# w_down of a SwiGLU layer as seven block products: hidden kept as seven pieces, half of the results added by accumulating transfers

## The chip, the cores and the metric

The kernel runs on one NeuronCore of a Trainium2 chip. The metric is the device time of one execution in microseconds (us), as a median of several runs. The engines are named as the profile names them: PE is TensorE (PEld its weight loads), DVE is VectorE, ACT is ScalarE, POOL is GpSimd, SP is SyncE, which here only starts DMA transfers.

## The reference, cut to what matters

One inference step of a hybrid encoder of two layers over 656 tokens, with a model width of 1024 and a feed-forward width of 2816, all in fp32. Each layer is a SwiGLU, a mixer (pooling, convolution, attention) and a second SwiGLU:

```python
def swiglu(x, w_gate, w_up, w_down):
    return (jax.nn.silu(x @ w_gate) * (x @ w_up)) @ w_down

h   = x + 0.5 * swiglu(rmsnorm(x, g1), ...)     # SwiGLU 1
h   = h + mixer(rmsnorm(h, gm))
out = h + 0.5 * swiglu(rmsnorm(h, g2), ...)     # SwiGLU 2
```

There are four SwiGLUs in all. The change concerns their last product, the one by `w_down` (2816 x 1024).

## The kernel before

**Layout.** Everything stands transposed: features on the 128 partitions, tokens along the free axis. The 656 tokens are worked in two halves of 328 (the last SwiGLU drops 16 tokens and has halves of 320). The feed-forward width is 22 tiles of 128, taken as 11 pairs; `H` holds the residual as 8 tiles `m` of 128 features.

**Products in fp32.** `mm3` makes one fp32 product from three matmuls in the faster fp32r format: each operand is split into a high and a low part (`split`: ACT copies the high part, DVE subtracts it to get the low one), and high times high, high times low and low times high are summed in PSUM. In the profile all these matmuls have one line, L143, and differ by the PSUM tile that they write: `mm` (2 buffers), `z` (4) or `aux` (2).

**Units.** The program is a list of units. Each loads weights into `raw` or `rawb` by SP's DMA queue, splits them into slabs (`prep_next`: ACT the high part, DVE the low one; a slab is 4 blocks of 128x128, hence the operations of 128x512), and runs matmuls. `pump`, called after each product, loads and splits ahead, as buffers come free. The order in which each engine then takes its instructions is set by a scheduler that simulates the time line.

**Gate and up** are pair units (`pair_unit`, `run_pair`). Two tiles of output features, two halves of the tokens and two halves of the 1024 inputs make a 2x2 by 2x2 block product, which is made in seven block products instead of eight, as Strassen and Winograd do: 7 x 12 = 84 matmuls. The seven combined inputs (`B11`, `B12`, `B21`, `B22`, `Q1`, `Q2`, `T3`, `T4`) stand in `XR`; `mix` makes the combinations with four DVE operations. The combined weights are made by two accumulating transfers (`grow`: a DMA that POOL issues and that adds to what its destination holds) and two DVE additions. Results are put together by ACT and DVE. The last product, `T4`, is not run in its own unit: `self.late` keeps it, and the next unit runs it behind its own first product.

**Down, before.** `w_down` is worked in four chunks of 2, 3, 3 and 3 pairs (`CHUNKS`). `up_out` multiplies silu(gate) by up and splits each tile of the hidden layer into `Ra` (in the profile `ra`): one split of 656 tokens for each of the pair's two tiles. When a chunk is complete, 8 plain units (`hu_down`, one for each `m`) each make, for each half of the tokens, one sum in a `z` bank over the chunk's tiles, 3 matmuls a tile, and DVE adds it to `H` (`H<-z`). The list puts a chunk's eight down units behind the next chunk's first gate unit:

```python
                units.append(self.pair_unit(g[l], f, self.gate_out))
                units += down
                down = []
                units.append(self.pair_unit(up[l], f, self.up_out, i=2 * i))
```

So the order is: ..., up unit of the chunk's last pair, gate unit of the next pair, the eight down units, up unit of that pair. The up unit's `T4`, on which the last hidden tile waits, runs within that gate unit. Behind it come `mul`, and the split of that tile.

## Time and profile before

| | |
|---|---|
| Runs | 2853.79, 2850.09, 2853.23 us, median 2853.23 us |
| The profiled execution | 2852.38 us, of which the trace's span is 2850.7 us |
| PE busy | 2821.5 us, 99% of the span |
| DVE busy | 1853.5 us, 65% |
| ACT busy | 1320.7 us, 46% |
| POOL busy | 222.5 us, 8% |
| PE's waits for other work | 26 us in 13 groups |
| Mean granted TensorE clock | 0.994 |

The share of an engine is its busy time by the span, and an average over stages. Matmuls are pipelined, and the mean of one that a group gives covers its whole passage (312 ns), which overlaps with its neighbours; what a matmul costs is a full stretch of PE by the number of matmuls in it.

### The profile page before, as it was taken

How to read it: one execution, taken by the hardware profiler on the slowest of the kernel's cores; microseconds unless marked ns; L12 is line 12 of the kernel's file. 1: busy time of each engine (PE TensorE's matmuls, PEld its weight loads, DVE VectorE, ACT ScalarE, POOL GpSimd, SP SyncE). 2: the span in 40 equal slices, each digit the busy share in tenths (PEclk: the TensorE clock that was granted, in tenths of full speed). 3: DMA queues.
4: the chain of work that ended last, by engine and by line, in shares of the span. 5: the costliest groups of instructions: out<-in, count | busy, mean ns of one | idle time of the engine just before them, and what ended most of it. 6: DMA issues, size and time to landing. Idle time of an engine off the chain costs nothing.

```text
span 2850.7 us, 48269 instructions
## 1 busy us (share of the span) xinstructions
PE 2821.5 (99%) x19179; PEld 2781.3 (98%) x19179; DVE 1853.5 (65%) x3422; ACT 1320.7 (46%) x2544; POOL 222.5 (8%) x321
## 2 busy tenths in 40 slices
PE   8999999999999999999999999999999999999999
PEld 7999999999999999999999999999999999999999
DVE  8676675876444776575776665758764456775764
ACT  6353454776333343353554443547763234443443
POOL 1001000011000001000010010001110001000010
PEclk8999999999999999999999999999999999999999
DMA  5445444222222445454445454442222225444452
GB/s 148 115 128 120 120 113 99 80 78 70 75 71 71 101 116 138 107 128 117 123 105 131 122 128 103 109 100 81 68 77 71 74 76 134 111 121 117 126 124 73
DMA packets 506772, 297.26 MB, mean 104 GB/s; under 512 B 14430, under 2 KB 481570, under 8 KB 506546
## 3 DMA queue, kind: packets, MB, share of 16 engines
q1 hardware_dynamic: 478692, 241.87, 29.5%
q0 software_dynamic: 27360, 51.98, 10.6%
q8 instruction: 150, 2.46, 0.3%
q14 instruction: 76, 0.62, 0.1%
q10 hardware_dynamic: 494, 0.32, 0.0%
HBM read 233.84 MB, written 8.31 MB: 85 GB/s over the span
## 4 chain that ended last, share of the span: by engine, by line
PE 96%; DMA 2%; DVE 1%; ACT 1%; issue 0%; POOL 0%; ACTq 0%; SPq 0%; DVEq 0%; POOLq 0%
PE z L143 59%; PE mm L143 36%; PE aux L143 1%; DMA Wa<-rawb 0%; DMA raw<-in_ffn_w_gate_dram 0%; DVE Wa L131 0%; DMA raw<-in_ffn_w_up_dram 0%; DVE XR L134 0%; PE aux L1088 0%; DMA rawb<-in_ffn_w_gate_dram 0%; DMA rawb<-rawb 0%; ACT Wa L120 0%; DVE ws L134 0%; PE aux L1068 0%; DMA Wa<-in_k_norm_dram 0%
## 5 line engine op out<-in xcount | busy, mean ns | idle before, releaser
L143 PE MATMUL mm<-XR,ws 128*128 128x328 f32 (+3 forms) x4848 | 800.8, 314 | 2.1 <-DVE Wa L134 2.1
L143 PEld LDWEIGHTS mm<-XR,ws 128*128 128x128 f32 x4848 | 738.6, 188 | 7.0 <-issue 2.9
L143 PE MATMUL z<-XR,ws 128*128 128x328 f32 (+3 forms) x3924 | 628.5, 312 | 7.5 <-ACT XR L120 6.6
L143 PEld LDWEIGHTS z<-XR,ws 128*128 128x128 f32 x3924 | 596.2, 189 | 9.0 <-ACT XR L120 7.2
L143 PE MATMUL z<-ra,ws 128*128 128x328 f32 (+1 forms) x2688 | 421.0, 311 | 1.4 <-DVE H L131 1.4
L120 ACT ACTIVATE ws<-raw 128x512 fp32r<-128x512 f32 (+1 forms) x429 | 264.2, 618 | 324.0 <-PE z L143 206.5
L143 PEld LDWEIGHTS z<-ra,ws 128*128 128x128 f32 x2688 | 405.1, 188 | 1.7 <-DVE H L131 1.7
L134 DVE TENSOR_TENSOR ws<-raw,ws 128x512 fp32r<-128x512 f32 (+1 forms) x429 | 287.9, 673 | 176.7 <-ACT ws L120 175.3
L143 PE MATMUL z<-ra,slabs 128*128 128x328 f32 (+1 forms) x2112 | 330.3, 312 | 0.0
L143 PEld LDWEIGHTS z<-ra,slabs 128*128 128x128 f32 x2112 | 319.3, 188 | 0.1
L143 PE MATMUL mm<-XR,slabs 128*128 128x328 f32 (+1 forms) x1944 | 316.4, 312 | 0.0
L143 PE MATMUL z<-XR,slabs 128*128 128x328 f32 (+1 forms) x1764 | 297.0, 315 | 7.3 <-DVE Wa L134 7.3
L143 PEld LDWEIGHTS mm<-XR,slabs 128*128 128x128 f32 x1944 | 296.5, 188 | 0.0
L143 PEld LDWEIGHTS z<-XR,slabs 128*128 128x128 f32 x1764 | 274.3, 191 | 8.0 <-DVE Wa L134 7.9
L134 DVE TENSOR_TENSOR Wa<-Wa 128x328 f32<-128x328 f32 (+5 forms) x325 | 215.2, 668 | 36.4 <-ACT Wa L120 33.0
L131 DVE SCALAR_TENSOR_TENSOR H<-z,H 128x328 f32<-128x328 f32 (+1 forms) x288 | 140.9, 493 | 143.5 <-PE z L143 143.2
L120 ACT ACTIVATE slabs<-raw 128x512 fp32r<-128x512 f32 (+1 forms) x183 | 109.4, 601 | 160.4 <-PE z L143 78.0
L120 ACT ACTIVATE Wa<-Wa 128x656 f32<-128x656 f32 (+7 forms) x232 | 136.9, 597 | 92.5 <-DVE Wa L134 88.6
L120 ACT ACTIVATE ws<-rawb 128x512 fp32r<-128x512 f32 (+1 forms) x183 | 109.5, 601 | 147.3 <-PE z L143 94.2
L120 ACT ACTIVATE Wa<-mm 128x328 f32<-128x328 f32 (+1 forms) x240 | 105.5, 439 | 148.9 <-PE mm L143 147.9
L120 ACT ACTIVATE slabs<-rawb 128x512 fp32r<-128x512 f32 (+1 forms) x181 | 107.6, 599 | 143.8 <-PE z L143 99.3
L134 DVE TENSOR_TENSOR ws<-rawb,ws 128x512 fp32r<-128x512 f32 (+1 forms) x183 | 118.8, 652 | 61.0 <-ACT ws L120 60.1
(177 smaller groups left out, 2552.8 us busy)
## 6 DMA issues: line engine op xcount, KB each, us to landing
raw<-in_w_in_dram SPq DMA_DIRECT2D x88, 512.0 KB, 3.7
raw<-in_ffn_w_gate_dram SPq DMA_DIRECT2D x57, 512.0 KB, 4.0
rawb<-in_ffn_w_up_dram SPq DMA_DIRECT2D x55, 512.0 KB, 4.5
rawb<-in_ffn_w_down_dram SPq DMA_DIRECT2D x48, 384.0 KB, 3.3
raw<-in_ffn_w_down_dram SPq DMA_DIRECT2D x48, 384.0 KB, 3.4
raw<-in_ffn_w_up_dram SPq DMA_DIRECT2D x33, 512.0 KB, 3.9
rawb<-in_ffn_w_gate_dram SPq DMA_DIRECT2D x31, 512.0 KB, 3.5
Wa<-in_ffn_w_gate_dram SPq DMA_DIRECT2D x40, 256.0 KB, 3.9
```

Of the source, the lines that this page charges most:

```text
L120: i = self.nc.scalar.activation(out, in_, func, **kw).ins
L131: return self.nc.vector.scalar_tensor_tensor(out, in0, scalar, in1, op0=op0, op1=op1).ins
L134: self.nc.vector.tensor_tensor(out, in0, in1, op=op)
L143: self.nc.tensor.matmul(out, lhsT, rhs, start=start, stop=stop, skip_group_check=True)
```

## The change

**Chunks.** There are five chunks, of 2, 2, 2, 2 and 3 pairs. The last is done as before. The `w_down` of the first four is done by seven block products.

**Down units.** For a chunk of two pairs, tiles `m` and `m + 4` of the output, the two halves of the tokens and the two tiles of each pair make the 2x2 by 2x2 blocks. A `down_unit` (four to a chunk, for m = 0 to 3) runs 7 products of 2 x 3 = 6 matmuls, 42 in all, in three banks, where two plain units for the same outputs ran 48. Its last product, `T4`, is kept as `late` too. Its weights are four SP transfers of 128 KB and one more (`a21`), two accumulating transfers, two DVE additions of 128x256, and slabs of 4, 4, 4 and 2 blocks.

**Results.** The two blocks of tile `m` are the sum of two banks each: ACT takes a bank times 0.5 into one of six buffers (`terms`), and an accumulating transfer adds that to `H` (`first`, four times a unit). The blocks for `m + 4` are added by DVE as before (`second`, with factor -0.5, three times a unit).

**Hidden.** Of each pair the hidden layer is kept as seven pieces. `up_out` does, when the pair is complete: a split of one block of 328, a split of two (656), `mix` (four DVE operations of 328), and a split of four blocks (1312), where there were two splits of 656.

The diff, cut to its core:

```diff
-CHUNKS = ((0, 2), (2, 3), (5, 3), (8, 3))
+CHUNKS = ((0, 2), (2, 2), (4, 2), (6, 2), (8, 3))
...
+    def down_unit(self, w, r0, l, m):
+        part = lambda r, m: w[r0:r0 + 4 * P, m * P:(m + 1) * P].rearrange("(i r p) c -> r p i c", r=2, p=P)[r]
+        parts = [(4 * c + 2 * r, 2, part(r, m + 4 * c)) for c in range(2) for r in range(2)]
+        return dict(slabs=[4, 4, 4, 2], src=[(KD, parts)], placed=True, prep=self.prep_down, then=self.sums_down,
+                    early=self.early_down, run=self.run_down, ring="F", s3n=1, m=m, l=l, a21=part(0, m + 4))
...
+    def early_down(self, u):
+        (_, A), = u["raw"]
+        self.nc.sync.dma_start(u["s3"], u["a21"])
+        self.grow(A[:, 4:6], A[:, 6:8])
+        self.grow(u["s3"], A[:, 0:2])
+
+    def sums_down(self, u, i):
+        if i == 1:
+            (_, A), = u["raw"]
+            self.tt(A[:, 0:2], A[:, 4:6], A[:, 0:2], ALU.add)
+            self.tt(A[:, 2:4], A[:, 0:2], A[:, 2:4], ALU.add)
...
+        def first(hi, bank):
+            t = self.terms[self.term_i % 6][:, :n]
+            self.term_i += 1
+            self.act(t, bank[:, :n], AF.Identity, scale=0.5)
+            self.grow(h[0][hi], t)
+
+        def second(hi, bank):
+            self.stt(h[1][hi], bank[:, :n], -0.5, h[1][hi], ALU.mult, ALU.add)
+
+        plain = self.use(u)
+        prod(b1, plain, 0, B11, True)
+        first(0, b1)
+        self.pump(1)
+        if self.late:
+            self.late()
+        s1 = self.use(u)
+        prod(b2, s1, 0, Q1, True)
+        second(1, b2)
...
+        prod(b3, plain, 1, B21, True)
+        first(0, b3)
...
+        prod(b1, s2, 0, Q2, False)
+        first(1, b1)
...
+        prod(b2, s2, 1, B22, False)
+        first(1, b2)
...
+        prod(b1, s3, 0, T3, False)
+        second(1, b1)
...
+        def last():
+            self.late = None
+            prod(b1, s1, 1, T4, False)
+            second(0, b1)
...
-            for m in SLOTS:
-                down.append(self.unit(k, [(0, k, dn[l][r0:r0 + k * P, m * P:(m + 1) * P])], self.hu_down, "F",
-                                      m=m, l=l, scale=0.5, to=to if ci == len(CHUNKS) - 1 else None,
-                                      last=ci == len(CHUNKS) - 1))
+            if final:
...
+            else:
+                down = [self.down_unit(dn[l], r0, l, m) for m in range(4)]
...
     def up_out(self, u, r, n):
         s, w = (a[:, 2 * n * r:2 * n * (r + 1)] for a in (self.sil, self.up))
         self.mul(w, w, s)
-        self.split(self.r_at(0, u["i"] + r, c.start, c.stop), self.r_at(1, u["i"] + r, c.start, c.stop), w)
+        b = [self.up[:, q * n:(q + 1) * n] for q in range(4)]
+        if r == (1 if "plain" in u else 0):
+            self.split(self.hid(0, i, B11, n), self.hid(1, i, B11, n), b[0])
+        if r:
+            self.split(self.hid(0, i, B21, n, 2), self.hid(1, i, B21, n, 2), w)
+            self.mix(*b)
+            self.split(self.hid(0, i, Q2, n, 4), self.hid(1, i, Q2, n, 4), self.up[:, :4 * n])
```

**Where it moves instructions.** The first place is PE, at the first chunk's down products in the first SwiGLU. `mm_735` (before) and `mm_741` (after) is the bank of the up unit's last product T4; `mm_856` and `mm_874` are banks of the gate unit that follows; rows with `ra_550` are down products. Before:

```order
L143 MATMUL mm_735<-XR,slabs_104 128x328 x12
L143 MATMUL mm_856<-XR,ws_815 128x328 x12
L143 MATMUL z_857<-XR,ws_835 128x328 x12
L143 MATMUL z_984<-ra_550,slabs_104 128x328 x9
L143 MATMUL z_1022<-ra_550,slabs_104 128x328 x2
L143 MATMUL mm_856<-XR,ws_853 128x328 x12
L143 MATMUL z_984<-ra_550,slabs_104 128x328
L143 MATMUL z_1022<-ra_550,slabs_104 128x328
L143 MATMUL z_984<-ra_550,slabs_104 128x328 x2
```

And after, again from T4 on:

```order
L147 MATMUL mm_741<-XR,slabs_104 128x328 x12
L147 MATMUL mm_874<-XR,ws_871 128x328 x12
L147 MATMUL mm_1018<-XR,slabs_104 128x328 x6
L147 MATMUL z_1020<-ra_550,slabs_104 128x328 x3
L147 MATMUL z_1094<-ra_550,ws_1013 128x328 x3
L147 MATMUL z_1095<-ra_550,ws_995 128x328 x3
L147 MATMUL z_1020<-ra_550,slabs_104 128x328
L147 MATMUL z_1095<-ra_550,ws_995 128x328
L147 MATMUL mm_874<-XR,slabs_104 128x328 x12
L147 MATMUL z_1020<-ra_550,slabs_104 128x328 x2
L147 MATMUL z_1095<-ra_550,ws_995 128x328 x2
L147 MATMUL mm_1018<-ra_550,slabs_104 128x328 x3
```

What follows right behind:

```order
L147 MATMUL mm_1093<-XR,ws_995 128x328 x6
L147 MATMUL mm_1093<-ra_550,ws_1029 128x328 x3
L147 MATMUL z_1019<-ra_550,slabs_104 128x328
L147 MATMUL mm_1018<-ra_550,slabs_104 128x328
L147 MATMUL z_1094<-ra_550,ws_1013 128x328
L147 MATMUL mm_1093<-ra_550,ws_1029 128x328
L147 MATMUL z_1019<-ra_550,slabs_104 128x328 x2
L147 MATMUL mm_1018<-ra_550,slabs_104 128x328 x2
L147 MATMUL z_1094<-ra_550,ws_1013 128x328 x2
```

Before, the first product that needs the newest low part of the hidden tile is the last row (`z_984` x2). After, the first that needs the newest pair's high parts of `mix` is the third row of the second piece (`z_1019`), and of its low parts the seventh. Between T4 and the row in question stand 49 matmuls before and 61 after (52 before the high part's row).

The second place is DVE, from the evict of the same T4 to the newest low part. Before:

```order
L131 SCALAR_TENSOR_TENSOR Wa<-mm_735,Wa 128x328
L134 TENSOR_TENSOR slabs_104<-rawb_105,slabs_104 128x512
L134 TENSOR_TENSOR Wa<-Wa 128x656
L134 TENSOR_TENSOR ra_550<-Wa,ra_550 128x656
L134 TENSOR_TENSOR Wa<-z_857,Wa 128x328
```

After, first half and second half:

```order
L135 SCALAR_TENSOR_TENSOR Wa<-mm_741,Wa 128x328
L138 TENSOR_TENSOR slabs_104<-rawb_105,slabs_104 128x512
L138 TENSOR_TENSOR Wa<-Wa 128x656
L138 TENSOR_TENSOR rawb_105<-rawb_105 128x256
L138 TENSOR_TENSOR ws_1029<-rawb_105,ws_1029 128x512
L138 TENSOR_TENSOR rawb_105<-rawb_105 128x256
L138 TENSOR_TENSOR ra_550<-Wa,ra_550 128x656
L138 TENSOR_TENSOR Wa<-Wa 128x328
L138 TENSOR_TENSOR slabs_104<-rawb_105,slabs_104 128x512
L138 TENSOR_TENSOR Wa<-Wa 128x328
```

```order
L135 SCALAR_TENSOR_TENSOR Wa<-Wa 128x328
L138 TENSOR_TENSOR Wa<-Wa 128x328
L135 SCALAR_TENSOR_TENSOR Wa<-mm_874,Wa 128x328
L138 TENSOR_TENSOR slabs_104<-Wa,slabs_104 128x256
L135 SCALAR_TENSOR_TENSOR Wa<-Wa 128x328
L138 TENSOR_TENSOR slabs_104<-raw_914,slabs_104 128x512
L135 SCALAR_TENSOR_TENSOR Wa<-Wa 128x328
L138 TENSOR_TENSOR raw_914<-raw_914 128x256
L138 TENSOR_TENSOR ws_1132<-Wa,ws_1132 128x256
L138 TENSOR_TENSOR raw_914<-raw_914 128x256
L138 TENSOR_TENSOR ra_550<-Wa,ra_550 128x1312
```

The newest low part is the last row with `ra_550`: the fourth instruction from T4's evict before, the twenty-first after, because the mix, the sums of the down units' weights and their splits now stand between.

The third place is POOL, which issues the accumulating transfers, in the same SwiGLU. Before, each pair unit's two are the only ones:

```order
L410 DMA Wa<-rawb_105 128x512
L410 DMA rawb_105<-rawb_105 128x512
L410 DMA Wa<-raw_1036 128x512
L410 DMA raw_1038<-raw_1038 128x512
L410 DMA Wa<-rawb_105 128x512
```

After, the down units' sums (128x256) and the results (`H<-Wa`) come in:

```order
L445 DMA Wa<-raw_922 128x256
L445 DMA raw_922<-raw_922 128x256
L445 DMA H<-Wa 128x328
L445 DMA rawb_105<-rawb_105 128x512
L445 DMA H<-Wa 128x328 x2
L445 DMA Wa<-rawb_105 128x512
L445 DMA H<-Wa 128x328 x6
L445 DMA Wa<-raw_1204 128x512
L445 DMA raw_1206<-raw_1206 128x512
L445 DMA H<-Wa 128x328 x7
```

A pair unit's transfers (128x512) now stand among 16 transfers into `H` a chunk, four for each of its four down units.

## Rows read from the trace of the kernel before

**Rows 1.** The page: busy time of each engine, and the granted clock in 40 slices

```profile
PE 2821.5 (99%) x19179; PEld 2781.3 (98%) x19179; DVE 1853.5 (65%) x3422; ACT 1320.7 (46%) x2544; POOL 222.5 (8%) x321
...
PEclk8999999999999999999999999999999999999999
```

**Rows 2.** The page: the chain that ended last, by engine and by line

```profile
PE 96%; DMA 2%; DVE 1%; ACT 1%; issue 0%; POOL 0%; ACTq 0%; SPq 0%; DVEq 0%; POOLq 0%
```

**Rows 3.** PE's waits: us in total, times, longest us

```profile
PE z L143 <- DVE Wa L134: 7.3, 2, 4.1
PE z L143 <- ACT XR L120: 6.6, 2, 5.5
PE aux L143 <- ACT Wa L120: 2.9, 1, 2.9
...
PE z L143 <- DVE H L131: 1.4, 1, 1.4
```

**Rows 4.** Windows over one chunk, its two parts, and chunks of other SwiGLUs

```profile
core 0: us, PE busy (x) PEld busy (x) DVE busy (x) ACT busy (x) POOL busy (x), PEclk, DMA share, GB/s
128.60:247.80 119.20, 119.20 (x795) 119.20 (x795) 76.76 (x134) 50.27 (x94) 9.41 (x11) 1.00 0.48 119
128.60:210.00 81.40, 81.40 (x544) 81.40 (x544) 61.63 (x104) 41.94 (x80) 5.98 (x7) 1.00 0.48 120
210.00:247.80 37.80, 37.80 (x253) 37.80 (x252) 15.12 (x30) 8.33 (x14) 3.43 (x4) 1.00 0.49 116
1098.30:1217.50 119.20, 119.20 (x794) 119.20 (x793) 77.22 (x134) 50.19 (x94) 9.53 (x11) 1.00 0.48 119
2505.40:2621.60 116.20, 116.20 (x795) 116.20 (x794) 76.33 (x133) 49.95 (x94) 9.55 (x11) 1.00 0.48 122
```

**Rows 5.** DVE's groups, shapes apart

```profile
L134 DVE TENSOR_TENSOR ws<-raw,ws 128x512 fp32r<-128x512 f32 x405 | 278.2, 688 | 174.2 <-ACT ws L120 172.8
...
L134 DVE TENSOR_TENSOR Wa<-Wa 128x656 f32<-128x656 f32 x130 | 108.7, 836 | 1.5
...
L131 DVE SCALAR_TENSOR_TENSOR H<-z,H 128x328 f32<-128x328 f32 x208 | 102.1, 495 | 94.1 <-PE z L143 94.0
...
L134 DVE TENSOR_TENSOR ra<-Wa,ra 128x656 fp32r<-128x656 f32 x66 | 55.2, 836 | 12.3 <-ACT ra L120 12.3
L134 DVE TENSOR_TENSOR Wa<-Wa 128x328 f32<-128x328 f32 x92 | 45.6, 496 | 26.6 <-ACT Wa L120 25.8
L131 DVE SCALAR_TENSOR_TENSOR Wa<-Wa 128x328 f32<-128x328 f32 x88 | 43.3, 493 | 0.4
...
L134 DVE TENSOR_TENSOR XR<-Wa,XR 128x1312 fp32r<-128x1312 f32 x8 | 12.2, 1519 | 0.2
...
L134 DVE TENSOR_TENSOR ws<-raw,ws 128x256 fp32r<-128x256 f32 x24 | 10.1, 419 | 2.5 <-ACT ws L120 2.5
```

**Rows 6.** ACT's groups, shapes apart

```profile
L120 ACT ACTIVATE ws<-raw 128x512 fp32r<-128x512 f32 x405 | 254.3, 629 | 308.5 <-PE z L143 198.0 <-PE mm L143 84.7 <-issue 8.7
...
L120 ACT ACTIVATE Wa<-mm 128x328 f32<-128x328 f32 x180 | 79.3, 441 | 110.8 <-PE mm L143 110.1
L120 ACT ACTIVATE ra<-Wa 128x656 fp32r<-128x656 f32 x66 | 49.4, 749 | 32.2 <-DVE Wa L134 32.1
...
L120 ACT ACTIVATE XR<-Wa 128x1312 fp32r<-128x1312 f32 x8 | 10.3, 1289 | 1.1 <-DVE Wa L131 1.1
```

**Rows 7.** DVE in order of time, behind the T4 of a chunk's last up unit

```profile
start us, us, engine line op out<-in xcount [idle before <-releaser]
...
197.31 0.50 DVE L131 SCALAR_TENSOR_TENSOR Wa<-mm,Wa 128x328 f32<-128x328 f32 x1 [0.61 <-PE mm L143]
197.85 0.84 DVE L134 TENSOR_TENSOR Wa<-Wa 128x656 f32<-128x656 f32 x1
198.61 0.68 DVE L134 TENSOR_TENSOR slabs<-rawb,slabs 128x512 fp32r<-128x512 f32 x1
199.52 0.84 DVE L134 TENSOR_TENSOR ra<-Wa,ra 128x656 fp32r<-128x656 f32 x1 [0.22 <-ACT ra L120]
...
200.98 0.49 DVE L134 TENSOR_TENSOR Wa<-z,Wa 128x328 f32<-128x328 f32 x1
201.39 0.41 DVE L134 TENSOR_TENSOR slabs<-raw,slabs 128x256 fp32r<-128x256 f32 x1
```

**Rows 8.** POOL's accumulating transfers: the issue, ns min/median/max

```profile
L410 POOL DMA_DIRECT2D Wa<-Wa x30: 841/864/1128, 444.5 to 2403.4; - x30
```

**Rows 9.** DMA issues: count, KB each, median us to landing

```profile
raw<-raw POOLq DMA_DIRECT2D x40, 256.0 KB, 3.2
Wa<-raw POOLq DMA_DIRECT2D x40, 256.0 KB, 4.1
...
Wa<-Wa POOLq DMA_DIRECT2D x24, 328.0 KB, 4.1
```

**Rows 10.** Windows of PE over gaps, and over the stretch behind each

```profile
core 0: us, PE busy (x), PEclk, DMA share, GB/s
1012.80:1017.00 4.20, 0.30 (x3) 1.00 0.52 94
1017.05:1020.40 3.35, 3.17 (x11) 0.50 0.00 0
110.50:112.20 1.70, 0.31 (x3) 1.00 0.40 68
112.20:115.60 3.40, 3.36 (x22) 1.00 0.43 77
2422.90:2426.40 3.50, 0.29 (x3) 1.00 0.41 75
2426.80:2430.10 3.30, 3.30 (x14) 0.50 0.00 0
```

More of the change, by code (lines that the diff above doesn't have):

```diff
@@ L205, in setup @@
         self.parts = W[:, o:o + 2624]
+        self.terms = [W[:, o + 656 + 328 * i:o + 656 + 328 * (i + 1)] for i in range(6)]
         o += 2624
@@ L212, in setup @@
         o += 2624
-        self.s3 = [W[:, o + 512 * i:o + 512 * (i + 1)] for i in range(2)]
+        self.s3 = W[:, o:o + 1024]
         self.sq_row = W[:, o:o + DM]
@@ L325, in load_next @@
             return False
+        if n3:
+            self.s3_busy[i3:i3 + n3] = [True] * n3
+            self.s3_i = (i3 + n3) % 4
+            u["s3i"] = i3
+            u["s3"] = self.s3[:, 2 * P * i3:2 * P * (i3 + n3)].rearrange("p (k c) -> p k c", k=2 * n3)
         u["raw"] = []
@@ L672, in ffn_ready, with new_hidden, hid @@
         self.ffn_raw()
-        self.Ra = self.sb.tile([P, 2, 6, T], F32R, tag="Ra", name=self.name("ra"))
+        self.new_hidden()
+    def new_hidden(self):
+        self.Rf = self.sb.tile([P, 12 * T], F32R, tag="Ra", name=self.name("ra"))
+        self.Ra = self.Rf.rearrange("p (s k c) -> p s k c", s=2, k=6)
+    def hid(self, s, i, q, n, blocks=1):
+        if q == B11:
+            return self.xs(s, i, B12, n)
+        o = (2 * i + s) * 6 * 328 + (q - B21) * n
+        return self.Rf[:, o:o + blocks * n]
@@ new lines, in down_unit, with run_down, prod @@
+    def down_unit(self, w, r0, l, m):
[3 more added lines that the diff above has]
+                    early=self.early_down, run=self.run_down, ring="F", s3n=1, m=m, l=l, a21=part(0, m + 4))
+    def run_down(self, u):
+        c0 = self.halves[0][0]
+        n = self.halves[0][1] - c0
+        b1, b2, b3 = self.psum("mm"), self.psum("z"), self.psum("z")
+        h = [[self.H[:, m, c0 + hi * n:c0 + (hi + 1) * n] for hi in range(2)] for m in (u["m"], u["m"] + 4)]
+        self.clock += 1
+        def prod(bank, slab, half, q, start):
+            w = slab[0][0]
+            for i in range(2):
+                k = 2 * half + i
+                self.mm3(bank[:, :n], w[:, 0, k, :], w[:, 1, k, :], self.hid(0, i, q, n), self.hid(1, i, q, n),
+                         start and i == 0, i == 1)
+        def first(hi, bank):
[14 more added lines that the diff above has]
+        second(1, b2)
+        self.pump(1)
+        prod(b3, plain, 1, B21, True)
+        self.used(plain)
+        first(0, b3)
+        self.pump(1)
+        s2 = self.use(u)
+        prod(b1, s2, 0, Q2, False)
+        first(1, b1)
+        self.pump(1)
+        prod(b2, s2, 1, B22, False)
+        self.used(s2)
+        first(1, b2)
+        self.pump(1)
+        s3 = self.use(u)
+        prod(b1, s3, 0, T3, False)
+        self.used(s3)
+        second(1, b1)
+        self.pump(1)
+        def last():
+            self.late = None
+            prod(b1, s1, 1, T4, False)
+            self.used(s1)
+            second(0, b1)
+            self.pump(1)
+        self.late = last
+        self.slot_tail()
@@ L689, in ffn_units @@
                 down = []
-                units.append(self.pair_unit(up[l], f, self.up_out, i=2 * i))
+                units.append(self.pair_unit(up[l], f, self.up_out, i=i, final=final))
             r0, k = 2 * f0 * P, 2 * fn
-            for m in SLOTS:
-                down.append(self.unit(k, [(0, k, dn[l][r0:r0 + k * P, m * P:(m + 1) * P])], self.hu_down, "F",
-                                      m=m, l=l, scale=0.5, to=to if ci == len(CHUNKS) - 1 else None,
-                                      last=ci == len(CHUNKS) - 1))
+            if final:
+                for m in SLOTS:
+                    down.append(self.unit(k, [(0, k, dn[l][r0:r0 + k * P, m * P:(m + 1) * P])], self.hu_down, "F",
+                                          m=m, l=l, scale=0.5, to=to, last=True))
+            else:
+                down = [self.down_unit(dn[l], r0, l, m) for m in range(4)]
         return units + down
@@ L1310, in build @@
         units[0]["after_it"] = self.load_consts
+        for i, u in enumerate(u for u in units if "turn" in u):
+            u["turn"] = i % 2
         self.run_units(units)
```

42 lines of the change are left out of this document (29 added, 13 removed).

## The prediction

> **What bounds the kernel now.** I read the busy shares first: PE is busy 99% of the span, DVE 65%, ACT 46%, POOL 8%, and the granted clock is at its upper level (2.4 GHz) nearly throughout [rows 1]. A share is only an average, so the chain that ended last comes next: 96% of it is PE [rows 2]. Then PE's waits: some 26 us in all, in a few places of 1 to 5 us [rows 3], and by their times none within the middle of a SwiGLU. The windows over one chunk settle it. From one chunk of three pairs to the next there are six pair units of 84 matmuls and eight down units of 36, so 504 + 288 = 792 matmuls; PE is busy for all of the 119.20 us in two SwiGLUs, and all of 116.20 us in the last one, which has fewer tokens [rows 4]. A matmul costs 119.20 / 792 = 0.1505 us, and 116.20 / 792 = 0.1467 us in the last SwiGLU. So in the stage that is changed each matmul left out gives its full time back, as long as DVE and ACT deliver; there DVE is busy 76.8 us of 119.2, and unevenly: 61.6 of 81.4 us among pair units, 15.1 of 37.8 us among down units [rows 4].
>
> **What it removes.** For a chunk of two pairs, four down units of 42 matmuls (168) stand where 48 matmuls for each of four pairs of `m` (192) would: 24 fewer. Four chunks in each of four SwiGLUs make 16 x 24 = 384, of which 96 are in the last SwiGLU. Gain: 288 x 0.1505 + 96 x 0.1467 = 43.3 + 14.1 = **57.4 us**.
>
> **What it adds off the path.** In `up_out` a pair cost two low parts of 656 on DVE (2 x 0.836) and costs now 0.50 + 0.84 + 1.52 for the low parts of one, two and four blocks and 4 x 0.49 for `mix`: 4.8 for 1.7, so 3.1 us more a pair [rows 5]. A down unit has on DVE the low parts of slabs (3 x 0.69 + 0.42), two sums of 0.42 and three additions to `H` of 0.495: 4.8 us of the unit's 42 x 0.1505 = 6.3 us. On ACT it has the high parts (3 x 0.63 + 0.42 at most) and four evicts of 0.44: 4.1 us [rows 6]. A chunk of two pairs takes 504 matmuls, 75.9 us, and DVE has some 61 to 65 us of work in it, 81 to 86% where it had 64%. It stays below PE on average, and that is the cover that hides all of this. It no longer does at one place in each chunk.
>
> **The wait that is added.** The down products need the newest pair's pieces, and these start only with T4 of the chunk's last up unit, which runs a unit late, within the next gate unit. Before, DVE goes from T4's evict at 197.31 over `mul` and a slab to the low part, which ends at 199.52 + 0.84 = 200.36: 3.05 us, against 49 matmuls (7.4 us) that PE has in the meantime. After, the same stretch of DVE's order has 21 instructions: eight of 328 elements, four of 512, six of 256, two of 656 and the low part of 1312. With the means of the groups: 8 x 0.495 + 4 x 0.688 + 6 x 0.419 + 2 x 0.836 + 1.519 = 12.4 us [rows 5]. Back-to-back DVE instructions overlap: one starts at 200.98 for 0.49 us, and the next at 201.39, so 0.08 us each [rows 7], which leaves 10.7. To it come waits for ACT: the high part of 1312 takes 1.29 us, and DVE fills only some of it; one mix operand waits on an evict (0.44) that queues on ACT behind a slab (0.63) [rows 6]. I put these at 1.7 us: the low part is ready 12.4 us after T4. PE's cover is 61 matmuls, 9.2 us. So PE waits **3.2 us**, and behind the waiting product all of PE's queue stands, the down units' own later products too.
>
> By the same count in the other 15 places the cover is 57 to 88 matmuls (8.6 to 13.2 us, less in the last SwiGLU), DVE's share 10.7 to 12.8 us, and the waits are 0 to 4.6 us: 3.2, 2.6, 3.2, 2.6 in the first SwiGLU, 1.1, 1.9, 4.6, 1.9 in the second, 0, 4.6, 1.9, 4.6 in the third, 1.0, 2.1, 4.5, 2.1 in the last. Their sum is **42 us**. Bounds: with 1.4 us less at each (ACT's waits nearly all covered) it is 22 us; with 1 us more at each (a slab of 0.69 and a wait in front, say) 58 us.
>
> **The clock.** After gaps of 3.5 and 4.2 us PE ran at half clock (1.2 GHz) for some 3.3 us; after one of 1.7 us it kept its clock [rows 10]. Half the rate over 3.4 us costs 1.7 us. Five of my waits are 4.5 us or longer, but each is broken by a few matmuls between the wait for the high and that for the low part. I take two falls, **3 us**; none gives 0, five give 8.5.
>
> **The accumulating transfers.** A down unit has POOL issue six (four into `H`, two for weights), each 0.864 us at the median [rows 8]: 5.2 us of 6.3. ACT's evict frees the bank at once, and six buffers of 128x328 cover one and a half units, 9.5 us. Two of a unit's four go into the same piece of `H` as two before, and the later must wait for the earlier to land. The scheduler interleaves two units on PE, so they are about 3.6 us apart; transfers of 256 and 328 KB took 3.2 to 4.1 us from issue to landing [rows 9], and mine have 164 KB. So POOL waits 0 to 1 us there, and with 5.2 us of issue it may fall behind 6.3 and in the end ACT waits for a buffer, and PE for a bank. There are 16 x 2 pairs of units, so the bounds are 0 and 32 us. I take **0**, since rows 9 suggest a landing below 3.6 us for a transfer half as large, and six buffers absorb the rest.
>
> The Trainium skill, "DMA: Bandwidth & Descriptors", section "Anatomy of one DMA — SWDGE (gpsimd) path", gives a fit of about 2.0 us plus the bytes by 436 KB a microsecond. For 256 to 328 KB that is 2.6 to 2.8 us (an estimate), less than the 3.2 to 4.1 us that the trace shows, so the two differ. By the page mine would land in 2.4 us (an estimate), and the hold below would not exist; the row leaves it open.
>
> **The sum.** Against the profiled execution: 2852.4 - 57.4 + 42 + 3 + 0 = **2840 us**. That execution lies 0.85 us under the median of 2853.2, which is less than its runs differ, so I leave it.
>
> **Rivals.**
> - *Hidden.* The wait isn't there or is under 1 us, since DVE's instructions go through faster than their means or PE's order gives other cover. For it: the cover of 88 matmuls in one place, and that DVE was never late in a chunk of before. Against it: 21 instructions on one engine in 9 us, counted from its own order. Then 2852.4 - 57.4 + 0 to 16 = 2795 to 2812 us.
> - *The other side: the newest pieces come later still.* The place is the same, the mechanism too: DVE or ACT enters the stretch with work in arrears (they are now at 81 to 86% over the chunk, and the pair units alone kept DVE at 61.63 of 81.4 us [rows 4]), so that the wait is 4 to 5 us, and the clock falls at each place. It decides from 57.4 / 16 = 3.6 us a place. With 3.6 to 4.4 us each, and 0 to 1 us of the clock's price on the mean, the time is 2853 to 2880 us. For it: four of my 16 waits are already 4.5 us and more (a fifth just at it). Against it: their mean is 2.6 us.
> - *The transfers hold.* POOL falls behind in the down stage, and the down units stretch beyond 6.3 us; the waits at the pieces remain. At 0 to 1 us a pair of units that adds up to 32 us: 2840 to 2870 us. The profile would show POOL busy or waiting throughout the stage.
>
> That the change does not do what it says is excluded: PE's order has 18,783 matmuls of this kind before and 18,399 after, the 384 fewer.
>
> **How the numbers follow.** My forecast (waits of 1 to 3.5 us a place) has 0.48, with its own range 2812 to 2848 us; hidden 0.14; later still 0.22; the transfers hold 0.16. The range reaches to the middle of hidden and to about that of the other side's: **2804 to 2868 us**, which leaves out some 0.07 of the one and 0.10 of the other. A measurement of this kernel can tell some 0.2% from no change, 5.7 us, so faster is below 2847.5 and slower above 2858.9. Faster: hidden, nearly all of the forecast, and little of the holding case, 0.62. Slower: most of the later-still case and part of the holding one, 0.20. Within: 0.18.
>
> **What would show it.** Right: PE's matmuls 384 fewer, and PE waiting at 16 places, twice each at most, on DVE and ACT instructions that write `ra`, for some 40 us; in the windows of a down stage DVE busy 70% and more, POOL 80%; few stretches at half clock. In between PE busy at 0.15 us a matmul. Wrong: waits of PE on `H` or on ACT's writes of `Wa` in the down stage (the transfers), or none on `ra` (hidden), or half clock behind all 16 places. Most of all I would be wrong if PE's order shifted the newest pieces' products against my count, since each 7 matmuls of cover are 1 us at 16 places.

## The result

The changed kernel takes **2955.6 us** (median of four runs, 2951.8 to 2957.8) against 2853.2 us: slower, ratio 1.036, 95% interval 1.034 to 1.038. The forecast was 2840 us, and the range ended at 2868.

What answers to [rows 1], the page of the changed kernel:

```profile
PE 2816.5 (95%) x18795; PEld 2753.1 (93%) x18795; DVE 2028.1 (69%) x3806; ACT 1494.2 (51%) x2928; POOL 557.8 (19%) x705
```

The 384 matmuls are gone (19,179 to 18,795), yet PE is busy only 5 us less, where 57 were removed: some of its work ran at half clock, and PE ran empty and filled again more often. The chain that ended last, which answers to [rows 2]:

```profile
PE 82%; DMA 7%; DVE 4%; issue 3%; ACT 2%; POOL 2%; ACTq 0%; POOLq 0%; SPq 0%; DVEq 0%
```

DMA and POOL are on it now. PE's waits, against [rows 3]:

```profile
PE mm L147 <- ACT Wa L124: 52.4, 21, 7.6
PE mm L147 <- DVE H L135: 20.2, 11, 6.5
PE mm L147 <- DVE Wa L135: 12.5, 12, 1.3
PE z L147 <- ACT ra L124: 11.5, 10, 1.7
PE z L147 <- ACT XR L124: 6.8, 2, 5.5
...
PE z L147 <- DVE ra L138: 7.3, 12, 0.9
PE z L147 <- DVE ws L138: 5.4, 2, 3.5
```

All rows together are 132 us, against 25 us before (the rows of before add up to 25.2, not to the 26 given above). Two kinds are new. The waits on `ra` (11.5 and 7.3) and those on `DVE Wa` (12.5), with a few short ones on `ACT Wa`, stand at the newest pieces, some 33 us, in the sixteen places that the prediction names. Those on `ACT Wa` (52.4), `DVE H` (20.2) and `DVE ws` (5.4), some 77 us, stand later, in the middle and at the end of the down stages. Each place by itself is seen in the order of time. PE at the first chunk of the first SwiGLU:

```profile
103.46 0.72 PE L147 MATMUL mm<-ra,ws 128*128 128x328 f32 x3 [0.70 <-ACT Wa L124]
104.95 0.42 PE L147 MATMUL z<-ra,slabs 128*128 128x328 f32 x1 [0.77 <-ACT ra L124]
105.21 0.31 PE L147 MATMUL mm<-ra,slabs 128*128 128x328 f32 x1
105.35 0.31 PE L147 MATMUL z<-ra,ws 128*128 128x328 f32 x1
105.50 0.31 PE L147 MATMUL mm<-ra,ws 128*128 128x328 f32 x1
106.51 0.57 PE L147 MATMUL z<-ra,slabs 128*128 128x328 f32 x2 [0.70 <-DVE ra L138]
```

Three waits in a row, on a bank, on the high parts and on the low parts: 2.2 us in all. T4's matmuls, and the low part that the third wait is for:

```profile
92.46 1.98 PE L147 MATMUL mm<-XR,slabs 128*128 128x328 f32 x12
...
104.93 1.53 DVE L138 TENSOR_TENSOR ra<-Wa,ra 128x1312 fp32r<-128x1312 f32 x1 [0.43 <-ACT ra L124]
```

T4 ended at 94.44 us, and the low part at 106.46: 12.0 us later, where 12.4 were forecast. From the first matmul behind T4 (94.27) to the one that needs the low part (106.51), PE took 12.24 us for 61 matmuls of 0.1505: 3.1 us were lost, the three waits and what PE needs to fill again behind each.

The other kind, ACT in the second chunk's down stage:

```profile
197.49 0.45 ACT L124 ACTIVATE Wa<-z 128x328 f32<-128x328 f32 x1 [0.52 <-PE z L147]
...
199.25 0.42 ACT L124 ACTIVATE ws<-Wa 128x256 fp32r<-128x256 f32 x1 [0.27 <-PE mm L147]
205.96 0.44 ACT L124 ACTIVATE Wa<-z 128x328 f32<-128x328 f32 x1 [6.29 <-DMA H<-Wa]
```

ACT stands for 6.29 us at one evict, since a transfer still reads the buffer that it wants; everything behind it on ACT, evicts of other banks and the splits of weights, stands too, and PE stops for 2.7 us. PE's row, and the row of all such waits of ACT:

```profile
207.31 2.01 PE L147 MATMUL mm<-ra,ws 128*128 128x328 f32 x6 [2.67 <-ACT Wa L124]
...
ACT Wa L124 <- DMA H<-Wa: 143.1, 31, 11.3
```

What POOL did meanwhile:

```profile
198.24 0.87 POOL L445 DMA_DIRECT2D H<-Wa  x1 [0.96 <-ACT Wa L124]
199.36 0.86 POOL L445 DMA_DIRECT2D H<-Wa  x1 [0.25 <-issue]
201.03 0.84 POOL L445 DMA_DIRECT2D H<-Wa  x1 [0.80 <-DMA H<-Wa]
202.88 0.85 POOL L445 DMA_DIRECT2D H<-Wa  x1 [1.01 <-issue]
```

The evict into the buffer in question began at 195.65, its transfer was issued at 201.03 and landed at 205.85. Taken over all 256 transfers of results, a term stood 4.2 us on average from its evict to the issue and 4.4 us from issue to landing, up to 20 us together. A chunk's 16 transfers took 45 us from the first issue to the last landing, on average; the stage's 168 matmuls take 25 us by themselves.

The clock adds to it: its mean is 0.980, against 0.994 before. By the clock's own records PE is granted the lower level of 1.2 GHz for 120 us, against 33 before. Of these 87 us more, 21 lie within PE's waits and cost nothing beyond them. In the rest matmuls start 0.27 us apart in place of 0.15; counted from their starts, that costs some 34 us. The sum of the spans: -57 (matmuls) + 107 (waits) + 34 (clock) = 84 of the 102.5 us. The refilling of PE after some 70 more waits adds 11 (a matmul passes in 0.31 us and is followed in 0.15, so 0.16 us each), and stalls too short to stand among the waits, under 0.15 us, some 12. That is 107, so it closes to within 5 us.

### The profile page after: what moved, and what is told of

Same layout as the page of the kernel before. It is cut to its first block, busy times and chain, and to the rows that moved or that the text cites. A ratio compares the mean times of both kernels' runs of the same rounds, so it can differ in the third digit from the quotient of the medians.

```text
span 2953.2 us, 49653 instructions
## 1 busy us (share of the span) xinstructions
PE 2816.5 (95%) x18795; PEld 2753.1 (93%) x18795; DVE 2028.1 (69%) x3806; ACT 1494.2 (51%) x2928; POOL 557.8 (19%) x705
## 4 chain that ended last, share of the span: by engine, by line
PE 82%; DMA 7%; DVE 4%; issue 3%; ACT 2%; POOL 2%; ACTq 0%; POOLq 0%; SPq 0%; DVEq 0%
PE z L147 44%; PE mm L147 36%; DMA H<-Wa 4%; POOL H L445 1%; ACT Wa L124 1%; DMA raw<-in_ffn_w_gate_dram 1%; DVE Wa L135 1%; PE aux L147 1%; DVE Wa L138 1%; DVE ra L138 1%; DVE slabs L138 1%; DVE ws L138 1%; DMA rawb<-in_ffn_w_up_dram 0%; ACT ws L124 0%; ACT ra L124 0%
## 5 line engine op out<-in xcount | busy, mean ns | idle before, releaser
L147 PE MATMUL z<-ra,ws 128*128 128x328 f32 (+1 forms) x1728 | 290.9, 314 | 4.1 <-ACT ra L124 3.2
L445 POOL DMA_DIRECT2D H<-Wa x256 | 230.3, 948 | 286.1 <-ACT Wa L124 117.3
L147 PEld LDWEIGHTS z<-ra,ws 128*128 128x128 f32 x1728 | 266.0, 189 | 6.8 <-ACT ra L124 4.2
L124 ACT ACTIVATE Wa<-mm 128x328 f32<-128x328 f32 (+1 forms) x368 | 160.0, 439 | 218.4 <-PE mm L147 205.3
L138 DVE TENSOR_TENSOR Wa<-Wa 128x656 f32<-128x656 f32 (+5 forms) x389 | 244.8, 638 | 15.8 <-ACT Wa L124 11.7
L124 ACT ACTIVATE Wa<-z 128x328 f32<-128x328 f32 (+4 forms) x280 | 124.3, 447 | 244.4 <-DMA H<-Wa 140.3
L147 PE MATMUL z<-ra,slabs 128*128 128x328 f32 (+1 forms) x1152 | 209.8, 322 | 15.5 <-ACT ra L124 8.4
L147 PEld LDWEIGHTS z<-ra,slabs 128*128 128x128 f32 x1152 | 185.6, 195 | 20.5 <-ACT ra L124 10.0
L138 DVE TENSOR_TENSOR slabs<-raw,slabs 128x512 fp32r<-128x512 f32 (+1 forms) x191 | 128.6, 674 | 82.0 <-ACT slabs L124 80.6
L138 DVE TENSOR_TENSOR Wa<-z,Wa 128x328 f32<-128x328 f32 (+1 forms) x224 | 109.8, 492 | 95.5 <-PE z L147 50.2
```

The lines of the kernel that those rows point to most:

```text
L124: i = self.nc.scalar.activation(out, in_, func, **kw).ins
L138: self.nc.vector.tensor_tensor(out, in0, in1, op=op)
L147: self.nc.tensor.matmul(out, lhsT, rhs, start=start, stop=stop, skip_group_check=True)
L445: self.nc.gpsimd.dma_start(to, by, accum_op=ALU.add)
```

## The experiments

Each time is compared with the kernel before, run beside it.

**No transfers.** The evicts stay; half of the results is not added to `H`.

```diff
             self.act(t, bank[:, :n], AF.Identity, scale=0.5)
-            self.grow(h[0][hi], t)
```

> Left out: the accumulating transfers of the down units' results; ACT still evicts each bank into its buffer, but half of the results is not added to H. Theory (the buffers come free too late, because the transfers wait for one another in POOL's queue and land after 4 to 5 us; ACT stands at the next evict, and PE behind it, and the clock falls): the 77 us of waits in the down stages and most of the 43 us of half clock go, the waits at the newest pieces (33 us) stay: 2825 to 2845 us. Rival (ACT's and DVE's load in the down stage, evicts and slabs, makes the waits, and the transfers are only what the wait is put down to): that load is all still there, so 2930 us or more.

2852.9 us, ratio 0.999 (0.998 to 1.000). The rival falls: 103 us come back without any work of ACT's or DVE's taken away. But the forecast of 2825 to 2845 falls too: without transfers the change gains nothing. PE's waits there:

```profile
PE mm L147 <- DVE Wa L135: 12.5, 12, 1.3
PE z L147 <- ACT ra L124: 11.6, 10, 1.7
PE z L147 <- DVE ra L138: 7.3, 12, 0.9
```

Of the new waits hardly any but those at the newest pieces are left. All waits are 60 us, 35 more than before; the refills (8), the short stalls (10) and some clock (6) make up the rest, and together they use up the whole gain.

**Early pieces.** Of a pair's seven pieces only B21 and T4 need the unit's product T4. In this version the other five are made as soon as T3 is evicted: `mul` of that block, B22's split, three of the four operations of `mix`, and the splits of Q2, Q1 and T3.

```diff
         self.stt(s[3], s[3], -1.0, f[:, n:], ALU.mult, ALU.mult)
+        if u.get("soon"):
+            self.up_soon(u, n)
...
+    def up_soon(self, u, n):
+        i = u["i"]
+        b = [self.up[:, q * n:(q + 1) * n] for q in range(4)]
+        self.mul(b[3], b[3], self.sil[:, 3 * n:4 * n])
+        self.split(self.hid(0, i, B22, n), self.hid(1, i, B22, n), b[3])
+        self.sub(b[3], b[3], b[1])
+        self.sub(b[1], b[0], b[1])
+        self.stt(b[0], b[0], -1.0, b[3], ALU.mult, ALU.subtract)
+        self.split(self.hid(0, i, Q2, n, 2), self.hid(1, i, Q2, n, 2), self.up[:, :2 * n])
+        self.split(self.hid(0, i, T3, n), self.hid(1, i, T3, n), b[3])
...
+            self.mul(b[2], b[2], self.sil[:, 2 * n:3 * n])
+            self.split(self.hid(0, i, B21, n), self.hid(1, i, B21, n), b[2])
+            self.stt(b[2], b[0], -1.0, b[2], ALU.mult, ALU.subtract)
+            self.split(self.hid(0, i, T4, n), self.hid(1, i, T4, n), b[2])
```

First without transfers, then with all of them:

> Left out: the transfers of the results, as in the run without them, so half of the results is not added to H. Besides, of a pair's seven pieces five are made as soon as T3 is there, and only the two that need T4 (B21 and T4) behind it. Theory (without transfers, the waits at the newest pieces are all that is left of the change's loss, 35 us of waits, 8 us for refilling PE's pipe and a few us more): 2795 to 2815 us. Rival (the down units are slower by themselves, by more work on DVE and ACT): 2835 us or more, as without the new order of the pieces.

2796.3 us, ratio 0.980 (0.978 to 0.982): 56 us, nearly the full gain. PE's longest waits are those that the kernel before has too; only the eleven short ones of the last row are new:

```profile
PE z L147 <- ACT XR L124: 6.6, 2, 5.5
PE aux L147 <- ACT Wa L124: 4.1, 2, 3.5
PE z L147 <- DVE Wa L138: 3.2, 1, 3.2
PE mm L147 <- ACT Wa L124: 3.0, 11, 0.5
```

> The changed kernel, transfers and all, with five of the seven pieces made as soon as T3 is there. Theory (two separate losses): the waits at the pieces go, those for the buffers stay, 2895 to 2925 us. Rival (one loss covers the other, so that PE waits for the transfers what it does not wait for the pieces): 2940 to 2965 us.

2890.2 us, ratio 1.013 (1.011 to 1.015), better than expected. So the two losses are separate: with transfers or without, late pieces cost 1.9 to 2.3% (55 to 65 us), and with late pieces or early ones, the transfers cost 3.3 to 3.7% (94 to 105 us).

The remaining runs look for what it is in the transfers.

**Who adds.** All results by DVE from the bank; or the first term of each piece of `H` by DVE and only the second by a transfer.

```diff
-            t = self.terms[self.term_i % 6][:, :n]
-            self.term_i += 1
-            self.act(t, bank[:, :n], AF.Identity, scale=0.5)
-            self.grow(h[0][hi], t)
+            self.stt(h[0][hi], bank[:, :n], 0.5, h[0][hi], ALU.mult, ALU.add)
```

> All results added to H by DVE straight from the bank, no buffers, no transfers of results. Theory: the waits for buffers go, but DVE has 6.8 us of work in a down unit of 6.3 us, so it is late by some 0.5 us a unit, 30 us in all, and the pieces' wait stays: 2835 to 2875 us. Rival (DVE's and ACT's load): DVE has more to do than after the change, 2960 us or more.

> Of the two terms of each piece of H the first is added by DVE from the bank, the second by ACT's evict and an accumulating transfer: two transfers a unit, and none waits for another one's landing. Theory: the six buffers then cover three units (19 us), more than a turn-round of 10 us, so the waits for buffers go; DVE has 5.8 us in 6.3: 2825 to 2860 us. Rival (any transfer into H that lands in 4 to 5 us holds ACT): about half of the loss stays, 2890 us or more.

All by DVE: 2898.8 us (1.016, 1.012 to 1.020), above its range: DVE is too late with slabs and pieces now, and half clock behind it is back. Half: 2878.9 us (1.009, 1.006 to 1.012), also above its range, with waits on the pieces as before.

**Half by DVE and early pieces.**

> A whole computation: the first term of each piece of H by DVE, the second by a transfer, and five of the seven pieces made as soon as T3 is there. Theory: neither of the two waits is left, DVE has 5.8 us in the 6.3 us of a down unit: 2805 to 2835 us, faster than both kernels. Rival (DVE becomes the bound in the down stage): 2855 us or more.

2820.0 us, ratio **0.989** (0.987 to 0.990): the whole computation, faster than both kernels by 33 and 136 us. Not all of the 57 us: waits of 37 us are left, against 25 before.

**Buffers.**

```diff
-            t = self.terms[self.term_i % 6][:, :n]
+            t = self.terms[self.term_i % 4][:, :n]
```

> Four buffers for the terms instead of six, nothing else. Theory: the turn-round of a buffer (about 10 us from evict to landing where I looked) now has to cover four evicts, so a down unit of 6.3 us is stretched towards 10 us: 60 to 200 us more than the changed kernel, 3015 to 3155 us. Rival (POOL's queue or ACT's load is what holds, not the buffers): within 15 us of the changed kernel's 2956 us.

> The changed kernel with seven buffers for the terms instead of six. Theory (a buffer's time from evict to landing, 8.6 us on average and up to 20 us, over the number of buffers is what holds ACT): four buffers cost 46 us more than six, so one more gives back some 12 to 25 us: 2930 to 2945 us. Rival (what stands ahead in POOL's queue sets the pace, however many buffers there are): 2950 us or more.

Four buffers: 3001.6 us, 46 more than six, less than expected. Seven (the last in the tail of the tile `rawb`): 2893.3 us (1.013, 1.010 to 1.016), 62 less than six, more than expected. A transfer there stays on its way about as long (4.6 us), and the buffer is bound longer (10.3 us against 8.6). But ACT is held for 72 us by the landing of results, in waits of 2.5 us on average, where it was 143 us in waits of 4.6; PE's waits on `ACT Wa` shrink, and the clock recovers to 0.993:

```profile
PE mm L147 <- ACT Wa L124: 19.7, 17, 4.5
PE mm L147 <- DVE Wa L135: 14.2, 15, 1.4
```

**Transfers into one piece apart**, by exchanging products so that the two into a piece of `H` are two issues apart:

```diff
+        s2 = self.use(u)
+        prod(b1, s2, 0, Q2, False)
+        first(1, b1)
+        self.pump(1)
         prod(b3, plain, 1, B21, True)
         self.used(plain)
         first(0, b3)
-        self.pump(1)
-        s2 = self.use(u)
-        prod(b1, s2, 0, Q2, False)
-        first(1, b1)
```

> The changed kernel with two products of a down unit exchanged (Q2 before B21), so that the two transfers into one piece of H stand two issues apart instead of one. Theory (a transfer that waits for the landing of the one before into the same piece holds POOL's whole queue, and so the turn-round of a buffer): a good part of the 77 us of waits and 43 us of half clock goes, 2880 to 2925 us. Rival (the landing of 4 to 5 us by itself, with six buffers, is what holds): 2940 to 2970 us.

2956.3 us (1.036): no effect, though POOL's waits on a landing of another transfer into `H` fell from 51 to 33 us. PE's waits moved from `ACT Wa` (14.1 us, for 52.4) to `DVE H` (61.9, for 20.2). The mechanism by which the prediction bounded the cost is not what makes it, at least not alone.

**Room for descriptors.**

```diff
-    nc = bacc.Bacc("TRN2", target_bir_lowering=False, num_devices=1, dynamic_dma_scratch_size=1024)
+    nc = bacc.Bacc("TRN2", target_bir_lowering=False, num_devices=1, dynamic_dma_scratch_size=2048)
```

> The changed kernel with twice the room for the descriptors of POOL's transfers (2048 for 1024 bytes a partition; two small constants share a tile, which makes the space). In the changed kernel POOL never had more than two transfers under way when it started another, and with three under way the next started 0.31 us after a landing: three under way, at 4.4 us each, are one transfer in 1.45 us, and a down unit of 6.3 us wants six. Theory (the room for descriptors bounds POOL's rate, and that holds the buffers, ACT and PE): more than three are under way, and the time comes near that without transfers (2849 us): 2850 to 2890 us. Rival (the landing of 4 to 5 us and the six buffers hold, or POOL's own issue time): 2935 to 2965 us.

> The whole computation as the change has it, with five of the seven pieces made as soon as T3 is there, and twice the room for descriptors. Theory: both losses gone, 2797 to 2830 us. Rival (landing or issue time hold): 2870 to 2895 us, as without the room.

> Half of the terms by DVE, early pieces, and twice the room for descriptors. Here two transfers a unit, with those of the weights four, need 5.8 us of the 6.3 at one in 1.45 us, so the room should matter little: 2805 to 2822 us against 2820 us without it. Rival (the room holds here too): below 2805 us.

2959.7, 2883.1 and 2827.4 us: no real effect in any; the last is 5 us above its range. The limit is real: POOL's idle time that no wait explains ("issue") fell from 60 to 21 us, and up to five transfers were under way where there were never more than three. But with more under way each landed later, 4.9 us on average for 4.4, and a buffer was bound as long, 8.6 us. The theory fell.

**Bytes and kind.** Half the columns of each transfer; plain copies in place of accumulating ones; plain copies issued by ACT itself.

```diff
-            self.grow(h[0][hi], t)
+            self.grow(h[0][hi][:, :n // 2], t[:, :n // 2])
```

```diff
-            self.grow(h[0][hi], t)
+            self.nc.gpsimd.dma_start(h[0][hi], t)
```

```diff
-            self.grow(h[0][hi], t)
+            self.nc.scalar.dma_start(h[0][hi], t)
```

> Left out: the second half of the columns of each accumulating transfer into H; the number of transfers, their order, waits and buffers are those of the changed kernel. Theory (the 16 DMA engines are full in the down stage: 85 to 97% busy where the kernel before has 49%; a unit asks for about 4 x 1.05 us of them for its results, 1.6 us for the weights' sums and 2.3 us for loads, 8.1 us in 6.3): the transfers' packets take half as long, 6.0 us a unit, and the waits for buffers mostly go; the waits at the pieces stay: 2855 to 2905 us. Rival (POOL's issue of 0.87 us each, or a landing that takes its time whatever the size): 2930 us or more.

> The changed kernel with plain copies in place of the accumulating transfers of results (left out: the addition to H, which is overwritten), on the same queue, in the same order, with the same bytes. Theory of the full DMA engines: an accumulating packet of 1312 bytes takes 0.135 us where loads move 512 bytes in 0.028 us, so a plain one should take about 0.07 us, and the result is near that with half of the columns: 2855 to 2905 us. Rival (the bytes or POOL's queue, not the addition): 2930 us or more.

> Plain copies of the terms into H (left out: the addition, H is overwritten), as in the run with plain copies, but issued by ACT itself right behind its evict instead of by POOL. Theory (a term waits 3.5 to 4.2 us in POOL's queue behind transfers that wait for something else, and this is what is left in the run with plain copies, 2895 us): 2845 to 2865 us, near the run without transfers (2849 us). Rival (the landing, or the DMA engines' load, is what is left): 2880 us or more.

2916.5, 2894.7 and 2919.9 us. With half of the bytes 39 of the 103 us come back, between the two expectations; with plain copies 61, within the range of the theory. The copies from ACT's queue came out as the rival says. The share of the DMA engines in some of the densest windows of the changed kernel's down stages, and last over a whole one, where [rows 4] have 0.49:

```profile
core 0: us, PE busy (x) PEld busy (x) DVE busy (x) ACT busy (x) POOL busy (x), PEclk, DMA share, GB/s
104.00:130.00 26.00, 20.08 (x123) 18.26 (x122) 13.43 (x25) 10.69 (x23) 12.28 (x15) 0.97 0.88 175
190.00:206.00 16.00, 13.60 (x87) 12.79 (x85) 9.98 (x20) 6.63 (x14) 6.88 (x8) 1.00 0.93 185
1106.00:1120.00 14.00, 14.00 (x94) 13.82 (x93) 8.01 (x18) 5.87 (x12) 6.82 (x8) 1.00 0.97 206
181.00:218.50 37.50, 32.96 (x205) 31.88 (x204) 25.53 (x48) 18.85 (x38) 14.64 (x17) 0.95 0.76 156
```

and with half the columns, and then with plain copies, one dense window and a whole stage each:

```profile
190.00:206.00 16.00, 14.13 (x89) 13.13 (x88) 11.43 (x23) 7.54 (x14) 6.35 (x8) 1.00 0.74 153
182.50:220.20 37.70, 33.16 (x205) 32.07 (x204) 25.55 (x48) 19.31 (x40) 15.76 (x19) 0.95 0.66 133
```

```profile
190.00:206.00 16.00, 16.00 (x101) 16.00 (x101) 10.76 (x21) 8.13 (x18) 6.69 (x11) 0.93 0.71 198
177.70:211.90 34.20, 32.57 (x205) 31.99 (x204) 25.64 (x48) 19.70 (x40) 11.76 (x19) 0.95 0.65 178
```

The same stage of the kernel that took 2820.0 us, with half of the transfers:

```profile
171.70:208.10 36.40, 36.31 (x242) 35.85 (x240) 32.17 (x65) 19.65 (x40) 11.22 (x13) 1.00 0.80 171
```

There the engines are as busy over the stage, 0.80, and PE hardly pauses, so a high share by itself doesn't make the loss. What the results take of the engines' time is seen in the pages' rows of POOL's queue, in the changed kernel, with half the columns, with plain copies, and without transfers:

```profile
q0 software_dynamic: 82656, 111.51, 23.6%
q0 software_dynamic: 82656, 90.15, 20.1%
q0 software_dynamic: 58080, 111.51, 18.5%
q0 software_dynamic: 45792, 68.77, 14.6%
```

Each share by its span gives 697, 586, 535 and 416 us. So the results take 281 us; half the columns takes away 40% of that and gives back 38% of the loss, plain copies take away 58% and give back 59%. As far as these two runs go, the loss follows the engines' time. But half the number of transfers (2878.9 us; 563 us of the engines, by its page's 19.6%) takes away 48% and gives back 75%, and a seventh buffer gives back 61% and takes away nothing. Plain copies change more than the engines' time, too: POOL issues one in 0.64 us on average, for 0.95, and has up to five under way.

PE's waits on `ACT Wa` are 34.2 and 20.6 us with half the columns and with plain copies, for 52.4. ACT's own queue did not help: a copy of 164 KB from it lands in 2.4 us (median of the 46 whose landing the trace tells), for 3.3 from POOL's, yet ACT's evicts are late (29.9 us of waits). ACT issues all 256 copies itself there, which is new work for it, so the run doesn't show what a term's wait in POOL's queue costs by itself.

**Sums of weights by POOL's own additions**, in the kernel that took 2820.0 us:

```diff
-        self.grow(A[:, 4:6], A[:, 6:8])
-        self.grow(u["s3"], A[:, 0:2])
+        self.nc.gpsimd.tensor_tensor(A[:, 4:6], A[:, 6:8], A[:, 4:6], ALU.add)
+        self.nc.gpsimd.tensor_tensor(u["s3"], A[:, 0:2], u["s3"], ALU.add)
```

> The whole computation: half of the terms by DVE, early pieces, and the two sums of a down unit's weights by POOL's own additions instead of accumulating transfers, so the DMA engines have 1.6 us less to do in a unit. Theory of the full DMA engines: below the 2820 us with transfers for these sums, 2803 to 2816 us. Rival (POOL's additions slow DVE, or are late themselves): 2820 us or more.

2846.8 us (0.997, 0.996 to 0.998): the rival. Two transfers a unit fewer, and slower by 27 us. POOL's additions take 0.95 to 1.22 us, and DVE's operations of 512 into `slabs` take 0.708 us in place of 0.685 (those of 256 from `Wa` 0.515 in place of 0.416). The Trainium skill, "SBUF — State Buffer", section "Who interferes with whom", says that a DVE instruction with two SBUF inputs contends with a GpSimd instruction that reads SBUF; the rows agree in kind, with 3% of the larger operation's time. That this makes the 27 us isn't shown; POOL's additions also stand in its queue until their weights are loaded.

**Early pieces and seven buffers.**

> The whole computation as the change has it, every result by the same transfers, with two repairs: five of the seven pieces made as soon as T3 is there, and seven buffers for the terms. Theory (the two losses are separate, and each repair gives what it gave alone, 65 and 62 us, less what both gave back of the clock): 2830 to 2850 us, faster than the kernel before. Rival (with the early pieces the down units run without a pause, so the buffers are bound as long and one more does not reach): 2865 us or more.

2911.3 us (1.020, 1.018 to 1.022): the rival again. Each repair alone gives some 63 us; together they give 44, 21 less than the early pieces alone. PE's waits are these:

```profile
PE mm L147 <- ACT Wa L124: 36.8, 16, 5.4
PE z L147 <- ACT Wa L124: 27.4, 10, 4.8
```

A chunk's 16 transfers take 43 us, much as with six buffers and with four (42 to 47 us in all runs with 16 full accumulating transfers). One more buffer lets PE go on somewhat longer, and then it waits for 4 to 5 us in one piece, and the clock falls (0.982). Waits of ACT, first in the changed kernel and then here:

```profile
ACT Wa L124 <- DMA H<-Wa: 143.1, 31, 11.3
ACT slabs L124 <- DMA raw<-raw: 11.6, 8, 2.7
```

```profile
ACT Wa L124 <- DMA H<-Wa: 43.2, 29, 6.5
ACT slabs L124 <- DMA raw<-raw: 61.6, 11, 9.7
```

So the buffers hold ACT little here. It stands at the split of weights whose sum (`raw<-raw`) has not landed; POOL issues these sums in the same queue as the results. With early pieces and six buffers that wait is 57.7 us already, with late pieces and seven 21.4. So what holds ACT has moved in good part from the results to the weights' sums among them in POOL's queue. This is read from the waits, no run tests it, and it doesn't say why the time is above that of the early pieces alone.

**The chunks alone**, in the kernel before:

```diff
-CHUNKS = ((0, 2), (2, 3), (5, 3), (8, 3))
+CHUNKS = ((0, 2), (2, 2), (4, 2), (6, 2), (8, 3))
```

> The kernel before with the five chunks of the change and nothing else of it. Theory (the chunks by themselves cost nothing): 2853 us within 6 us. Rival (an addition to H for two pairs instead of three, and so a fifth more of DVE's additions, is late somewhere): 2860 us or more.

2856.2 us, ratio 1.001 (1.000 to 1.002): the chunks cost nothing that matters.

## Why the prediction was wrong, step by step

- **The gain, 57.4 us: right.** The run without transfers and with early pieces returns it, 0.980 of 2852.7 us, which is 56 us.
- **The wait at the newest pieces, 42 us: right in place and mechanism, size a little high in the waits and low in the cost.** 33 us of waits in all, 2.2 us in the first place, where with the refills 3.1 us were lost for 3.2 worked out; the low part came 12.0 us after T4 for 12.4 forecast. Only 19 us of them are put down to `ra`; the others are on banks, most of them banks that DVE empties in the same stretch of its order (`DVE Wa L135`), which the prediction did not count; they are gone too where the pieces are made early. The loss by the late pieces is 55 to 65 us, since each wait also empties PE's pipe, and a few lower the clock. (The prediction counts five waits of 4.5 us and more; its own list has four, which changes neither the sum nor the range.)
- **The accumulating transfers, 0 us: the step that failed.** They cost 94 to 105 us. The prediction set POOL's issue time (5.2 us) against the unit's 6.3, and took the landing to be "below 3.6 us for a transfer half as large". Measured: 4.0 us for 164 KB, hardly less than the 4.1 us of 328 KB in [rows 9], and a term had stood as long before it was issued. Six buffers of 9.5 us were thought to absorb the rest; a buffer was bound 8.6 us on average and up to 20. What was never compared is the train of a whole chunk, 45 us for 16 transfers, with the 25 us in which the stage wants them. The bound of 32 us was too low as well: the waits alone are 77 us. The sign that the prediction gave for this case, waits of PE on `H` and on ACT's writes of `Wa`, is what the profile shows. By the Trainium skill, "DMA: Bandwidth & Descriptors", section "Anatomy of one DMA — SWDGE (gpsimd) path", 164 KB would land in 2.4 us (an estimate by its fit); the trace has 4.0.
- **The clock, 3 us: wrong with it.** Some 34 us (the 43 us in the expectations count time within waits twice). There were 22 stretches of the lower level, where the kernel before has 5. At or behind 14 of the 16 waits of 2.6 us and more, the start of the kernel left out, stands such a stretch of 3.4 to 10.2 us, as in [rows 10]; six more stand behind waits of 1.7 to 2.5 us. At the newest pieces there are three, where the prediction took two: the clock's part there was right, and the rest came with the waits for buffers.
- **DVE and ACT off the path: right while the rest holds.** In the run without transfers and with early pieces DVE is 73% busy, and it costs next to nothing. In the down stage of the changed kernel DVE has 62% and POOL 43% (window from 190 us), not the 70 and 80% forecast: they wait too.
- **The rival on the other side** had the wrong mechanism (pieces still later); the one named "the transfers hold" had the right place, and 2870 us as its end. Its time was 86 us too low.

**What stays open.** That the transfers of results cost 94 to 105 us is shown by leaving them out, and that fewer, smaller or plain ones cost less, by runs. What makes the train of a chunk's transfers 45 us long isn't settled. For the load of the DMA engines speaks that half the bytes and plain copies gave back the loss in step with the engines' time that they took away; against it as the only cause speak the seventh buffer, the half number of transfers, and a stage at 0.80 in which PE hardly pauses. Waiting for one piece and room for descriptors are excluded as the single cause, each by a run. POOL's queue is not, since the run that goes around it gives ACT the issuing. Why one more buffer helps with late pieces and harms with early ones was read from the waits, not tested.

## What to carry to other kernels

Count a handed-off result by its whole round: evict, wait for issue, landing, buffer free; and compare the train of all of a stage's transfers with the stage, not one transfer with one unit. When a result of one product gates seven pieces, ask which piece really needs it: making five of the seven earlier was worth some 60 us here, as much as the change was meant to bring. And weigh a wait by its length: with late pieces and seven buffers, 87 waits of 90 us together left the clock at 0.993; with early pieces and seven, 51 waits of 100 us took it to 0.982.

## What the runs showed of the hardware

An accumulating transfer of 164 KB between places in SBUF landed 4.0 us after its issue (median), one of 328 KB in 4.2, one of 82 KB in 3.4, and those of 128 KB between weights in 2.6 to 3.1. So the size says little of the time in these rows, which were taken under different load of the engines. A plain copy of 164 KB landed in 2.4 us from ACT's queue (median of 46) and in 3.3 from POOL's (one of 160 KB in 3.8 from either). A packet of 1312 bytes took 0.135 us of a DMA engine on average when it accumulated, and a plain one 0.059 from ACT's queue. POOL had at most three accumulating transfers under way with 1024 bytes a partition for descriptors, and with three under way the next started 0.31 us after a landing; with 2048 there were up to five or six, and each took longer. At the lower level of the clock matmuls of 328 columns started 0.27 us apart, at the upper 0.15.
